# Cutting the last loads of a mean over rows into six runs of columns across two rows, in place of seven within them

## The chip, the cores and the metric

The kernel runs on one core of a Trainium2 chip. The metric is the device time of one execution in microseconds (us). Times below are medians of several executions with their lowest and highest; "span" is the stretch from the first to the last instruction of a profiled execution, some 1.3 us shorter than the time of the same execution.

In the lines of profiles DVE is VectorE, ACT is ScalarE and SPq is the queue of SyncE, which issues the loads; L93 is line 93 of the kernel. A line of a timeline has the start and the length in us, the instruction, and in brackets how long its engine had been idle and what ended that. A **landing** is the moment at which the last semaphore update of a load arrives. Where a landing or a signal is given below to a thousandth, or from "the semaphore updates", it is read from the packed trace (trace.npz): no view prints it.

## The reference

```python
def setup_inputs():
    return {"x": np.random.randn(64, 256, 8192).astype(np.float32)}

def reference(x):
    return np.mean(x, axis=2)
```

These are 16,384 rows of 8192 numbers, 537 MB, read once. The output has 64 KB.

## The kernel before

The rows are taken in 64 blocks. In each, a partition holds two rows next to each other, 16,384 columns or 64 KB, so a block is 8 MB. Three slots in SBUF, the memory on the core, take turns. VectorE sums each block with one instruction. From block 62 on ScalarE helps: it sums the second row of block 62 with an ACTIVATE, its instruction for work element by element, whose accumulator gathers the sum.

Block 63, the last, is loaded in pieces, so that little is left to do when the last bytes come. The first row is one load, the second is cut into six:

```python
LAST_CHUNKS = (4096, 2048, 1024, 512, 256, 256)
ACT_FROM = 512
...
ld = load(xl[:, 0, :], x_l[:, 0, :], tail_sem[0])
dve_sum(head[:, 0:1], xl[:, 0, 0:half])._wait_ge(tail_sem[0], 16)
act_sum(head[:, 1:2], xl[:, 0, half:S])._wait_ge(tail_sem[0], 16)

pos, k = 0, 0
for c, w in enumerate(LAST_CHUNKS):
    last = c == len(LAST_CHUNKS) - 1
    dst = fin_in[:, 0:w] if last else xl[:, 1, pos : pos + w]
    sem = tail_sem[c + 1]
    with tc.issue_after(ld.ins):
        ld = load(dst, x_l[:, 1, pos : pos + w], sem)
    if not last:
        wv = w // 2 if w >= ACT_FROM else w
        # VectorE sums the first wv columns, ScalarE the others, each into
        # a column of fin_in of its own
        ...
```

The last piece goes to `fin_in`, where the partial sums of the second row stand behind it. One **closing sum** over both gives that row's mean. It waits for ScalarE's signal (a drain that raises a semaphore) and for the last landing:

```python
with tc.issue_after(by_act.ins):
    nc.scalar.drain().then_inc(act_sem, 1)
...
scaled_sum(tail_out[:, RUN - R : RUN - 1], head[:])   # the head's scaled sum
...
by_dve = nc.vector.wait_ge(act_sem, 1)
...                                                   # and wait_ge(sem, 16), the last landing
scaled_sum(tail_out[:, RUN - 1 : RUN], fin_in[:, 0 : lastw + k])   # the closing sum
...
last_store = nc.sync.dma_start(out=out_tail, in_=tail_out[:])
```

## Time and profile before

| what | before | from |
|---|---|---|
| time | 1245.04 us (1244.99 to 1245.32, 3 runs) | the runs |
| span | 1244.0 us | page |
| input stream | 536.87 MB at 432 GB/s over the span | page |
| VectorE busy | 1087.1 us, 87% | page |
| start of block 62's sums | 1222.07 us | timeline |
| start of the closing sum | 1241.97 us | timeline |

A trace's absolute times carry all that happened in the 1220 us before. So I measure the end of the kernel as **distances from the start of block 62's sums**, which follow that block's landing by 0.02 us: 1241.97 - 1222.07 = 19.90 us to the closing sum. The last stretch of the chain of waits, whose columns are start, length and what ran:

```profile
1201.94 38.51 DMA xt<-in_x_dram
...
1240.48 1.47 DVE fin_in L93 x3
...
1241.97 0.12 DVE fin_in L99
```

The chain runs over the fourth of the last loads to VectorE's three last short sums and to the closing sum (L99). A chain merges instructions that follow each other closely.

### The profile page before, as it was taken

To read this page: it belongs to the slowest core of one execution; us is meant where nothing else is said; L and a number is where in the kernel's file an instruction comes from. 1 tells how busy PE (TensorE), PEld (TensorE's weight loads), DVE (VectorE), ACT (ScalarE), POOL (GpSimd) and SP (SyncE) were. 2 spreads that over 40 slices of the span, in tenths; PEclk is the share of its full clock that TensorE was granted. 3 is DMA by queue.
4 is the path that set the end of the run, shared out by engine and by line. 5 is a ranking of instruction groups with operands and counts; after the bars stand their busy time and mean duration, and the time that the engine had idled before them with its cause. 6 is when DMAs were issued, how large, how long until landed. Compare 5 with 4: busy or idle time off the path is not lost.

```text
span 1244.0 us, 207 instructions
## 1 busy us (share of the span) xinstructions
PE 0.6 (0%) x2; PEld 0.2 (0%) x2; DVE 1087.1 (87%) x76; ACT 16.4 (1%) x13; POOL 0.7 (0%) x6
## 2 busy tenths in 40 slices
PE   0000000000000000000000000000000000000000
PEld 0000000000000000000000000000000000000000
DVE  2898988989889889898898988989889898898988
ACT  0000000000000000000000000000000000000004
POOL 0000000000000000000000000000000000000000
DMA  9999999999999999999999999999999999999998
GB/s 436 407 438 438 438 438 436 407 438 438 438 438 438 436 407 438 438 438 438 438 436 407 438 438 438 438 438 436 407 438 438 438 438 438 434 411 436 438 438 373
DMA packets 10295, 536.95 MB, mean 432 GB/s; under 512 B 1278, under 2 KB 1590, under 8 KB 1846
## 3 DMA queue, kind: packets, MB, share of 16 engines
q1 hardware_dynamic: 10294, 536.94, 99.9%
q14 instruction: 1, 0.01, 0.0%
HBM read 536.87 MB, written 0.07 MB: 432 GB/s over the span
## 4 chain that ended last, share of the span: by engine, by line
DMA 70%; DVE 29%; SPq 0%; issue 0%; DVEq 0%
DMA xt<-in_x_dram 70%; DVE res L93 26%; DVE tail L93 3%; DVE fin_in L93 0%; SPq L83 0%; DVEq L188 0%; DVE fin_in L99 0%
## 5 line engine op out<-in xcount | busy, mean ns | idle before, releaser
L93 DVE TENSOR_REDUCE res<-xt 128x2 f32<-128x16384 f32 x56 | 964.4, 17221 | 139.4 <-DMA xt<-in_x_dram 139.4
L93 DVE TENSOR_REDUCE tail<-xt 128x2 f32<-128x16384 f32 (+1 forms) x7 | 112.0, 16001 | 13.8 <-DMA xt<-in_x_dram 13.8
L96 ACT ACT_TABLE_LOAD x1 | 1.3, 1283 | 1181.3 <-DVE tail L93 1181.3
L96 ACT ACTIVATE xt<-xt 128x8192 f32<-128x8192 f32 (+5 forms) x6 | 14.7, 2443 | 43.9 <-DMA xt<-in_x_dram 43.7
L93 DVE TENSOR_REDUCE fin_in<-xt 128x1 f32<-128x256 f32 (+3 forms) x5 | 5.0, 1006 | 0.5 <-DMA xt<-in_x_dram 0.4
L93 DVE TENSOR_REDUCE head<-xt 128x1 f32<-128x4096 f32 x1 | 4.4, 4420 | 0.7 <-DMA xt<-in_x_dram 0.7
L160 PE MATMUL ps<-ident,res 128*56 128x128 f32 x2 | 0.6, 404 | 1104.0 <-DVE res L93 1104.0
L96 ACT ACTIVATION_READ_ACCUMULATOR xt<-xt 128x1 f32 x6 | 1.1, 186 | 0.0
L161 DVE TENSOR_SCALAR bulk<-ps 56x128 f32<-56x128 f32 x2 | 0.5, 284 | 0.6 <-PE ps L160 0.6
L99 DVE TENSOR_SCALAR_CACHE_REDUCE fin_in<-fin_in 128x265 f32<-128x265 f32 x1 | 0.4, 431 | 0.0
L160 PEld LDWEIGHTS ps<-ident,res 128*56 128x56 f32 x2 | 0.2, 129 | 1104.0 <-issue 1104.0
L65 POOL TENSOR_SCALAR_AFFINE_SELECT ident<-ident 128x128 f32<-128x128 f32 x1 | 0.3, 292 | 0.1
L99 DVE TENSOR_SCALAR_CACHE_REDUCE head<-head 128x2 f32<-128x2 f32 x1 | 0.2, 155 | 0.1
L164 DVE TENSOR_SCALAR tail_out<-tail 128x14 f32<-128x14 f32 x1 | 0.2, 175 | 0.1
L64 POOL MEMSET ident<- 128x128 f32 x1 | 0.2, 204 | 0.3 <-POOLq L283 0.3
L283 POOL MEMSET const-bfloat16-1.0<- 128x1 bf16 x1 | 0.1, 101 | 0.0
L283 POOL MEMSET const-uint8-127<- 128x1 uint8 x1 | 0.1, 101 | 0.0
L283 POOL MEMSET const-float32-0.0<- 128x1 f32 x1 | 0.1, 98 | 0.2 <-issue 0.2
L283 POOL MEMSET const-float32-1.0<- 128x1 f32 x1 | 0.1, 98 | 0.0
L99 DVE DVE_READ_ACCUMULATOR head<-head 128x1 f32 x1 | 0.1, 84 | 0.0
L99 DVE DVE_READ_ACCUMULATOR fin_in<-fin_in 128x1 f32 x1 | 0.1, 83 | 0.0
## 6 DMA issues: line engine op xcount, KB each, us to landing
xt<-in_x_dram SPq DMA_DIRECT2D x1, 4096.0 KB, 31.1
xt<-in_x_dram SPq DMA_DIRECT2D x1, 2048.0 KB, 35.7
xt<-in_x_dram SPq DMA_DIRECT2D x1, 1024.0 KB, 37.7
xt<-in_x_dram SPq DMA_DIRECT2D x63, 40.8
xt<-in_x_dram SPq DMA_DIRECT2D x1, 512.0 KB, 38.5
xt<-in_x_dram SPq DMA_DIRECT2D x1, 256.0 KB, 38.7
xt<-in_x_dram SPq DMA_DIRECT2D x1, 128.0 KB, 38.6
fin_in<-in_x_dram SPq DMA_DIRECT2D x1, 128.0 KB, 38.5
```

Of the source, the lines that this page charges most:

```text
L64: nc.gpsimd.memset(ident[:], 0.0)
L65: nc.gpsimd.affine_select(out=ident[:], in_=ident[:], compare_op=mybir.AluOpType.not_equal, fill=1.0, base=0, pattern=[[-1, P]], channel_m ...
L93: return untracked(nc.vector.tensor_reduce(out=dst, in_=src, axis=X, op=ADD))
L96: return untracked(nc.scalar.activation(out=src, in_=src, func=COPY, accum_out=dst))
L99: return nc.vector.tensor_scalar(out=src, in0=src, scalar1=inv, scalar2=None, op0=mybir.AluOpType.mult, op1=ADD, accum_out=dst,)
L160: nc.tensor.transpose(out=ps[:TB, :], in_=res[:, r, :], identity=ident[:])
L161: nc.vector.tensor_scalar_mul(out=bulk[:TB, :, r], in0=ps[:TB, :], scalar1=inv)
L164: nc.vector.tensor_scalar_mul(out=tail_out[:, 0 : RUN - R], in0=tail[:], scalar1=inv)
L283: nc = _bacc.Bacc("TRN2", target_bir_lowering=False, num_devices=1)
```

## The change

The last block is cut as one run of 16,384 columns over both rows. The first of six pieces takes the first row whole and 960 columns of the second. A second number for each piece now says how many columns are VectorE's, and VectorE's share is smaller than before. The intent is one load less and less for VectorE to do at the end.

```diff
-LAST_CHUNKS = (4096, 2048, 1024, 512, 256, 256)
-
-ACT_FROM = 512
+LAST_CHUNKS = ((9152, 960), (3968, 1984), (1792, 896), (896, 256), (320, 320), (256, 256))
+HEAD = 3072
 ...
-    x_l = x_t[LB - TB]
-    ld = load(xl[:, 0, :], x_l[:, 0, :], tail_sem[0])
-    dve_sum(head[:, 0:1], xl[:, 0, 0:half])._wait_ge(tail_sem[0], 16)
-    act_sum(head[:, 1:2], xl[:, 0, half:S])._wait_ge(tail_sem[0], 16)
 ...
+        if c == 0:
+            dve_sum(head[:, 0:1], xl[:, 0:HEAD])._wait_ge(sem, 16)
+            act_sum(head[:, 1:2], xl[:, HEAD:S])._wait_ge(sem, 16)
+            assert wv == w - S
+        part = fin_in[:, lastw + k : lastw + k + 2]
+        mid = pos - w + (S if c == 0 else 0) + wv
+        dve_sum(part[:, 0:1], xl[:, mid - wv : mid])._wait_ge(sem, 16)
+        k += 1
+        if mid < pos:
+            by_act = act_sum(part[:, 1:2], xl[:, mid:pos])
 ...
```

More of the change, by code (lines that the diff above doesn't have):

```diff
@@ L39 @@
     TB = NB - RUN // R
-    assert SLOTS <= TB <= P and sum(LAST_CHUNKS) == S
+    assert SLOTS <= TB <= P and sum(w for w, _ in LAST_CHUNKS) == R * S
     inv = 1.0 / float(S)
-    half = S // 2
     x_f = x.rearrange("b c s -> (b c) s")
@@ L57 @@
     act_sem = tc.alloc_semaphore("act")
-    tail_sem = [tc.alloc_semaphore(f"tail{i}") for i in range(len(LAST_CHUNKS) + 1)]
+    tail_sem = [tc.alloc_semaphore(f"tail{i}") for i in range(len(LAST_CHUNKS))]
     res = pool.tile([P, R, TB], F32)
@@ L124 @@
     nparts = 2 * len(LAST_CHUNKS)
-    lastw = LAST_CHUNKS[-1]
-    xl = slots[LB % SLOTS]
+    lastw = LAST_CHUNKS[-1][0]
+    xl = slots[LB % SLOTS][:].rearrange("p r s -> p (r s)")
+    x_l = x_t[LB - TB].rearrange("p r s -> p (r s)")
     fin_in = nc.alloc_sbuf_tensor("fin_in", [P, lastw + nparts], F32)
     head = pool.tile([P, 2], F32)
-    x_l = x_t[LB - TB]
-    ld = load(xl[:, 0, :], x_l[:, 0, :], tail_sem[0])
-    dve_sum(head[:, 0:1], xl[:, 0, 0:half])._wait_ge(tail_sem[0], 16)
-    act_sum(head[:, 1:2], xl[:, 0, half:S])._wait_ge(tail_sem[0], 16)
     pos, k = 0, 0
-    for c, w in enumerate(LAST_CHUNKS):
+    for c, (w, wv) in enumerate(LAST_CHUNKS):
+        sem = tail_sem[c]
         last = c == len(LAST_CHUNKS) - 1
-        dst = fin_in[:, 0:w] if last else xl[:, 1, pos : pos + w]
-        sem = tail_sem[c + 1]
+        dst = fin_in[:, 0:w] if last else xl[:, pos : pos + w]
         with tc.issue_after(ld.ins):
-            ld = load(dst, x_l[:, 1, pos : pos + w], sem)
-        if not last:
-            wv = w // 2 if w >= ACT_FROM else w
-            part = fin_in[:, lastw + k : lastw + k + 2]
-            dve_sum(part[:, 0:1], xl[:, 1, pos : pos + wv])._wait_ge(sem, 16)
-            k += 1
-            if wv < w:
-                by_act = act_sum(part[:, 1:2], xl[:, 1, pos + wv : pos + w])
-                by_act._wait_ge(sem, 16)
-                tc.add_to_no_dep_group("act", by_act.ins)
-                k += 1
-        pos += w
+            ld = load(dst, x_l[:, pos : pos + w], sem)
+        pos += w
+        if last:
+            break
+        if c == 0:
[8 more added lines that the diff above has]
+            by_act = act_sum(part[:, 1:2], xl[:, mid:pos])
+            by_act._wait_ge(sem, 16)
+            tc.add_to_no_dep_group("act", by_act.ins)
+            k += 1
     with tc.issue_after(by_act.ins):
```

## The prediction

> **What bounds the kernel now.** I read the page first (busy shares, the 40 slices, the issues with their landing times), then the chain of waits for the last 60 us, then the timeline of the last 22 us. On the page these lines matter:
>
> ```profile
> DVE  2898988989889889898898988989889898898988
> ...
> GB/s 436 407 438 438 438 438 436 407 438 438 438 438 438 436 407 438 438 438 438 438 436 407 438 438 438 438 438 436 407 438 438 438 438 438 434 411 436 438 438 373
> ...
> HBM read 536.87 MB, written 0.07 MB: 432 GB/s over the span
> ...
> L93 DVE TENSOR_REDUCE res<-xt 128x2 f32<-128x16384 f32 x56 | 964.4, 17221 | 139.4 <-DMA xt<-in_x_dram 139.4
> ```
>
> The input stream runs at 436 to 438 GB/s in nearly every slice and never rests, while VectorE waits before each of its 56 large sums: 139.4 us of idle, all put down to the load (the first 21.8 us of it is the start). The load stream bounds the kernel. The change touches only the last block of 16,384 columns, which is 1/64 of it. Everything up to the landing of the block before it is built as now; the first of the last loads is issued when a slot is freed at 1200.62 us, far ahead of its turn. So the question is only the distance from the landing of the last whole block to the last store.
>
> ```profile
> xt<-in_x_dram SPq DMA_DIRECT2D x1, 4096.0 KB, 31.1
> xt<-in_x_dram SPq DMA_DIRECT2D x1, 2048.0 KB, 35.7
> xt<-in_x_dram SPq DMA_DIRECT2D x1, 1024.0 KB, 37.7
> ...
> xt<-in_x_dram SPq DMA_DIRECT2D x1, 512.0 KB, 38.5
> xt<-in_x_dram SPq DMA_DIRECT2D x1, 256.0 KB, 38.7
> xt<-in_x_dram SPq DMA_DIRECT2D x1, 128.0 KB, 38.6
> fin_in<-in_x_dram SPq DMA_DIRECT2D x1, 128.0 KB, 38.5
> ```
>
> These seven are issued within 3 us and then wait 31 to 39 us for their turn: issue time is hidden altogether. In the timeline:
>
> ```profile
> 1222.07 7.03 ACT L96 ACTIVATE xt<-xt 128x8192 f32<-128x8192 f32 x1 [39.46 <-DMA xt<-in_x_dram]
> ...
> 1231.79 3.62 ACT L96 ACTIVATE xt<-xt 128x4096 f32<-128x4096 f32 x1 [2.60 <-DMA xt<-in_x_dram]
> 1231.79 4.42 DVE L93 TENSOR_REDUCE head<-xt 128x1 f32<-128x4096 f32 x1 [0.75 <-DMA xt<-in_x_dram]
> ...
> 1236.35 0.15 DVE L99 TENSOR_SCALAR_CACHE_REDUCE head<-head 128x2 f32<-128x2 f32 x1
> ...
> 1236.69 2.29 DVE L93 TENSOR_REDUCE fin_in<-xt 128x1 f32<-128x2048 f32 x1 [0.18 <-DMA xt<-in_x_dram]
> ...
> 1241.52 0.42 DVE L93 TENSOR_REDUCE fin_in<-xt 128x1 f32<-128x256 f32 x1
> 1241.97 0.43 DVE L99 TENSOR_SCALAR_CACHE_REDUCE fin_in<-fin_in 128x265 f32<-128x265 f32 x1
> 1242.33 0.08 DVE L99 DVE_READ_ACCUMULATOR fin_in<-fin_in 128x1 f32 x1
> 1242.44 0.36 SPq L182 DMA_DIRECT2D out_dram<-tail_out  x1
> ```
>
> Each number at the left is a start in us. An engine starts some 0.02 us after the landing that it waits for, so landings can be read off: block 62 at 1222.05, the row at 1231.77, then 1236.67, 1239.17 and 1240.45 (the starts at 1236.69, 1239.19 and 1240.48). The last three, issued at about 1202.4, 1202.9 and 1203.36, land by the page at 1241.1, 1241.5 and 1241.86. The closing sum starts at 1241.97: after the last landing at 1241.86, and after VectorE's last short sum ends at 1241.94. **So the stream and VectorE are tied at the end to within 0.1 us.** From that start to the end of the span are 2.03 us (1244.0 - 1241.97): the sum, the store and its landing. The change doesn't touch those.
>
> **What the Trainium skill says.** "DMA: Bandwidth & Descriptors", section Specifications, gives a fabric ceiling of 435 GB/s for the 16 engines. The trace agrees: 438 GB/s in an undisturbed slice, and 8.389 MB in 19.36 us (433 GB/s) between two block landings. The same page, section "Anatomy of one DMA", splits a transfer into a fixed part of about 2 us, mostly the receipt of the last write, and bytes over 436 GB/s. The trace shows that fixed part hidden where loads stand behind each other: 7 loads took 1241.86 - 1222.05 = 19.81 us, and 16,384 columns at the block rate (below) are 19.28, so each load adds 0.076 us. "VectorE: DVE Perf Modes", the section on the TRN2 errata, says that an operation on SBUF pays a fixed latency for every instruction, measured there as about 150 cycles, and the section on perf-mode tiers gives tensor_reduce no fast mode. The trace agrees: 8192, 4096, 2048, 1024, 512 and 256 columns took 8686, 4420, 2286, 1220, 686 and 420 ns, which is 153 + 1.0417 per column. For ScalarE (7030, 3616, 1910, 1057, 629, 416 ns) I fit 203 + 0.8333 per column, and its accumulator read ends some 0.09 us after the ACTIVATE.
>
> **The change part by part.**
>
> *The stream.* It takes away one load and moves no byte less. With a fixed 0.076 us per load, a block of one load in 19.36 us gives (19.36 - 0.08)/16,384 = 1.177 ns per column. Starting from 1222.05, the new landings are: 9152 columns 10.77 + 0.08, at 1232.89; 3968 columns 4.67 + 0.08, at 1237.64; 1792 at 1239.82; 896 at 1240.95; 320 at 1241.41; 256 at 1241.79. Only the last one can set the end, and it comes 0.07 us earlier than now. That is all that the stream gives.
>
> *VectorE.* The first piece now lands 1.12 us later than the row did, so both engines begin later. In exchange VectorE gets 3072 + 960 + 1984 + 896 + 256 + 320 = 7488 columns in six sums in place of 8192 in six: 704 columns less, 0.73 us less. Step by step: 3072 columns take 3.35 us, 1232.91 to 1236.26; 960 take 1.15, to 1237.4; the scaled sum of the two head parts waits for ScalarE (below), some 0.2 us, to about 1237.75; 1984 columns take 2.22, to 1239.97; 896 take 1.09, to 1241.05; 256 take 0.42, to 1241.45; 320 (landed 1241.41) take 0.49, to 1241.91. The closing sum has 264 columns in place of 265 (8 parts, not 9): no change. Now VectorE is done at 1241.94; afterwards at about 1241.91.
>
> *ScalarE.* It has 5120 + 1984 + 896 + 640 = 8640 columns in four instructions in place of 7936 in five. 5120 take 4.47 us from 1232.91, and with the read are done at 1237.47; 1984 from 1237.66 are done at 1239.6; 896 from 1239.84 at 1240.9; 640 from 1240.97 take 0.74 and are done at 1241.80. Now it is done at 1241.66. The signal to VectorE follows through a drain whose length no view here shows; at 0.1 us (my assumption) it is there by 1241.9.
>
> *The sum.* The last landing moves from 1241.86 to 1241.79, VectorE from 1241.94 to 1241.91, ScalarE's signal from about 1241.76 to 1241.90. The closing sum starts after the last of them, at about 1241.94 in place of 1241.97. The gain is 0.03 us, less than the 0.33 us between the three runs of before (1244.99 to 1245.32). I predict **1245.0 us**, against 1245.04.
>
> **The rivals.**
>
> 1. *The head's scaled sum stands ahead of the 960-column sum on VectorE.* The order of instructions on an engine isn't simply the program's: in the trace the head's scaled sum, written after the loop, stands directly behind the head sum. Now that costs nothing, because ScalarE's half ends (1235.5) before VectorE's (1236.21). After the change ScalarE's part ends at 1237.47, 1.2 us after VectorE's 3072 columns. Were the order kept, VectorE would idle there to 1237.55, and all that follows would run late: 1.15 + 2.22 + 1.09 + 0.42 + 0.49 from about 1237.75 ends near 1243.05, so the kernel takes 1.1 us longer, some 1246.1. Against it: the 960-column sum has its data with the head's, comes earlier in the program, and ready work ought to be placed ahead of work that still waits. I give it about one in seven.
>
> 2. *ScalarE becomes the bound.* Its last part has grown from 256 to 640 columns. If its drain takes 0.3 us in place of 0.1, the closing sum starts at 1242.1 to 1242.2: the time is 1245.2. For it: its slack is the smallest of the three. It can't be large, as now the signal is there no later than 0.31 us after the read (1241.66 to 1241.97).
>
> 3. *The pieces flow at another rate.* The new pieces begin at odd offsets (column 9152 is byte 36,608 of a row pair) and all but the last are of other lengths than before; should the stream lose 5% from the second piece on (7232 columns, 8.5 us), it costs 0.4 us, some 1245.4. Against it: in the old pieces, from 128 KB to 4 MB, the rate was the same to within what 0.076 us per load explains. The opposite, that each load saved is worth more than 0.076 us (a full completion wait), is refuted by the landings just read.
>
> No route leads to 2% (25 us): the whole stretch from the last whole block's landing to the end is 1244.0 - 1222.05 = 22 us, 19.3 of which are bytes that must come anyway.
>
> **Range and chances.** The small terms (stream, engines, drain) make 1244.9 to 1245.3, the scatter of runs adds some 0.2 to 0.4 either way, and rival 1 alone lies outside. So 1244.5 to 1245.8 should hold it 8 times in 10. Faster by over 2%: 0.003; slower by over 2%: 0.007, for something not thought of; within 2%: 0.99.
>
> **What would show it right or wrong.** The 4 steps show as follows. The landing of the first piece: a start of VectorE and ScalarE at about 1232.9 us, 10.85 after block 62's; the last load lands 19.74 us after block 62, not 19.81. The durations: 3353, 1153, 2220, 1086, 420 and 486 ns on VectorE and 4470, 1856, 950 and 736 on ScalarE. The order: the 960-column sum directly behind the 3072-column one, and the head's scaled sum after it with less than 0.3 us of idle. The tie: the closing sum within 0.15 us of 19.9 us after block 62's landing. An idle gap of over 1 us on VectorE between its first and second sum of the block, a stretch between two landings over 3% longer than its columns times 1.177 ns plus 0.076 us, or a closing sum held over 0.2 us behind both VectorE's last sum and the last landing would prove the corresponding step wrong.

## The result and the profile after

| | before | after |
|---|---|---|
| time, same rounds | 1245.03 us (1244.93 to 1245.32, 6 runs) | 1245.10 us (1244.84 to 1245.65, 6 runs) |
| span | 1244.0 | 1243.5 |
| start of block 62's sums | 1222.07 | 1221.66 |
| first landing's sums after that | 9.72 | 10.85 |
| closing sum after that | 19.90 | 19.89 |
| store issued after that | 20.37 | 20.36 |

The ratio is 1.0001, with a 95% interval of 0.9988 to 1.0013. A ratio here is the mean time of one kernel's runs over that of the other's in the same rounds, so not quite the ratio of the medians.

The span fell by 0.5 us, but 0.41 of it lies before block 62's sums, where both kernels execute the same instructions. It is scatter of the stream. The rest lies in the last store, which took 1.5 us to land in this trace of before, and 1.4 after and in the repeat of before. In the 13 traces the start of block 62's sums lies anywhere from 1221.60 to 1222.30 us. The distance from there to the closing sum repeats to 0.01 us in both kernels (below), so that is the measure for all that follows.

The issues on the changed kernel's page (size, then us from issue to landing):

```profile
xt<-in_x_dram SPq DMA_DIRECT2D x1, 4576.0 KB, 32.3
xt<-in_x_dram SPq DMA_DIRECT2D x1, 1984.0 KB, 36.7
...
xt<-in_x_dram SPq DMA_DIRECT2D x1, 896.0 KB, 38.4
xt<-in_x_dram SPq DMA_DIRECT2D x1, 448.0 KB, 39.0
xt<-in_x_dram SPq DMA_DIRECT2D x1, 160.0 KB, 39.0
fin_in<-in_x_dram SPq DMA_DIRECT2D x1, 128.0 KB, 38.8
```

There are six loads, issued as early as the seven were, so issue time is hidden as before. Its timeline:

```profile
1232.51 4.47 ACT L96 ACTIVATE xt<-xt 128x5120 f32<-128x5120 f32 x1 [3.73 <-DMA xt<-in_x_dram]
1232.51 3.35 DVE L93 TENSOR_REDUCE head<-xt 128x1 f32<-128x3072 f32 x1 [1.88 <-DMA xt<-in_x_dram]
1235.78 1.14 DVE L93 TENSOR_REDUCE fin_in<-xt 128x1 f32<-128x960 f32 x1
...
1237.11 0.15 DVE L99 TENSOR_SCALAR_CACHE_REDUCE head<-head 128x2 f32<-128x2 f32 x1 [0.18 <-ACT xt L96]
...
1240.58 0.74 ACT L96 ACTIVATE xt<-xt 128x640 f32<-128x640 f32 x1
...
1241.03 0.49 DVE L93 TENSOR_REDUCE fin_in<-xt 128x1 f32<-128x320 f32 x1
...
1241.55 0.43 DVE L99 TENSOR_SCALAR_CACHE_REDUCE fin_in<-fin_in 128x264 f32<-128x264 f32 x1
```

Both engines wait longer for the first piece: 1.88 us on VectorE in place of 0.75. The 960-column sum stands directly behind the head's, and the head's scaled sum comes after it with 0.18 us of idle. Two lines decide the end. The 320-column sum starts at 1241.03: the sum ahead of it started at 1240.58, took 0.42 and ended at 1241.00, and the 320 columns, issued at 1202.00, landed at about 1241.0 (39.0 us on the page; 1241.002 by the semaphore updates). As a sum whose data are there starts before the one ahead has ended (shown below), it is the landing that set this start. ScalarE's 640 columns end at 1240.58 + 0.74 = 1241.32.

Where did the stream's gain go? The first 16,128 columns of the block are there in both kernels when VectorE's last short sum starts. In before, with six loads, that sum starts 1241.52 - 1222.07 = 19.45 us after block 62's; after, with five loads, 1241.03 - 1221.66 = 19.37. So the stream is **0.08 us** ahead. But that sum has 320 columns in place of 256 and takes 0.486 us in place of 0.420, which is **0.07 us** more. It leaves 0.01. What held the end wasn't the last landing: by the semaphore updates it comes at 1241.815 in before (19.75) and at 1241.315 after (19.66), 0.16 and 0.24 us ahead of the closing sum. That isn't all slack, as a wait needs time too: where ScalarE's signal came last (e_four_pieces below), 0.10 us passed from its semaphore update to the closing sum. If a landing needs as long or longer, the last one had at most some 0.06 us to spare in before and 0.14 after (an estimate from these figures).

My theory then: the end is the **landing of the last piece but one and one short sum on VectorE**, with ScalarE's signal close by. The rivals: VectorE's total work sets the end (it has no slack); or the stream's last landing does, and with it the number of loads.

### The profile page after: what moved, and what is told of

Its sections match the earlier page's. It is cut to its first block, busy times and chain, and to the rows that moved or that the text cites. A ratio compares the mean times of both kernels' runs of the same rounds, so it can differ in the third digit from the quotient of the medians.

```text
span 1243.5 us, 204 instructions
## 1 busy us (share of the span) xinstructions
PE 0.6 (0%) x2; PEld 0.2 (0%) x2; DVE 1086.3 (87%) x76; ACT 16.8 (1%) x11; POOL 0.7 (0%) x6
## 4 chain that ended last, share of the span: by engine, by line
DMA 70%; DVE 29%; issue 0%; SPq 0%; DVEq 0%
DMA xt<-in_x_dram 70%; DVE res L93 26%; DVE tail L93 3%; SPq L83 0%; DVE fin_in L93 0%; DVEq L188 0%; DVE fin_in L99 0%
## 5 line engine op out<-in xcount | busy, mean ns | idle before, releaser
L96 ACT ACTIVATE xt<-xt 128x8192 f32<-128x8192 f32 (+4 forms) x5 | 15.0, 3009 | 43.7 <-DMA xt<-in_x_dram 43.6
L93 DVE TENSOR_REDUCE fin_in<-xt 128x1 f32<-128x960 f32 (+4 forms) x5 | 5.3, 1071 | 0.1
L93 DVE TENSOR_REDUCE head<-xt 128x1 f32<-128x3072 f32 x1 | 3.4, 3352 | 1.9 <-DMA xt<-in_x_dram 1.9
```

The lines of the kernel that those rows point to most:

```text
L93: return untracked(nc.vector.tensor_reduce(out=dst, in_=src, axis=X, op=ADD))
L96: return untracked(nc.scalar.activation(out=src, in_=src, func=COPY, accum_out=dst))
```

## The experiments

Eleven kernels ran on the chip, each correct. Here is what they came to; "distance" is from the start of block 62's sums to that of the closing sum.

| kernel | distance | time, us | before in the same rounds |
|---|---|---|---|
| before_again | 19.90 | 1245.04 (1 run) | 1245.24 |
| after_again | 19.89 | 1245.24 | 1245.24 |
| e_head_first | 20.54 | 1245.70 | 1245.24 |
| e_even_split | 20.46 | 1245.86 | 1245.23 |
| e_eight_cuts | 20.77 | 1245.92 | 1245.24 |
| e_four_cuts | 20.03 | 1245.16 (1 run) | 1245.06 |
| e_two_cuts | 19.90 | 1245.00 | 1245.06 |
| e_act_late | 20.04 | 1245.63 (1 run) | 1245.23 |
| e_aligned | 19.97 | 1245.20 | 1245.23 |
| e_four_pieces | 21.13 | 1246.33 | 1245.23 |
| e_retuned | 19.83 | 1245.08 | 1245.06 |

### Both kernels again

No edit. Expected of the kernel before:

> The kernel before, once more, for the scatter of the measure used below: the distance from the start of block 62's sums to the start of the closing sum on VectorE, 19.90 us in its first trace (1241.97 - 1222.07). Theory (the end of the kernel is fixed by the last block alone, and the absolute times differ by the stream before it): again 19.87 to 19.93, while the start of block 62's sums itself may move by some tenths. Rival (the tail itself scatters by tenths): outside of that, and then no difference of 0.01 us between the two kernels means anything.

Expected of the changed one:

> The changed kernel once more, timed in five rounds. Theory: the distance from block 62's sums to the closing sum is 19.89 again (19.86 to 19.92), the last load lands 19.6 to 19.75 after them, and the time is within 0.3 us of before. Rival (the last landing's move shows in the time): faster by 0.1 us or more, in all rounds.

The distances came out as 1241.75 - 1221.85 = 19.90 and 1241.97 - 1222.08 = 19.89, the very values of the first traces, though the starts of block 62's sums had moved by -0.22 and +0.42 us. VectorE's last short sum started at 19.44 and 19.35, so the 0.08 or 0.09 of the stream repeats too. The changed kernel took 1245.24 us (1244.74 to 1245.39, 5 runs) beside 1245.24 (1244.86 to 1245.42, 9 runs), ratio 1.0 (0.9986 to 1.0013). The difference of 0.01 us in the tail is steady in the traces, and no count of rounds here would find it in the time.

### Has VectorE slack? The head's scaled sum ahead of the 960-column sum

```diff
+        if c == 0:
+            head_sum = scaled_sum(tail_out[:, RUN - R : RUN - 1], head[:])
         part = fin_in[:, lastw + k : lastw + k + 2]
 ...
-        dve_sum(part[:, 0:1], xl[:, mid - wv : mid])._wait_ge(sem, 16)
+        with tc.issue_after(head_sum.ins):
+            dve_sum(part[:, 0:1], xl[:, mid - wv : mid])._wait_ge(sem, 16)
 ...      # and the head's scaled sum behind the loop is gone
```

> The changed kernel with the head's scaled sum forced ahead of the 960-column sum on VectorE. Theory (VectorE has next to no slack between the first piece and the end): it idles until ScalarE's 5120 columns are done, some 15.45 us after block 62's sums, and then 1.14 + 2.22 + 1.09 + 0.42 + 0.49 us follow without a gap, so the closing sum starts 20.96 us after block 62's sums, 1.07 later than in the changed kernel; the time rises by about 1.1 us (0.7 to 1.4). Rival (the stream sets the end and VectorE has slack): less than 0.3 us.

Its timeline:

```profile
1237.11 0.15 DVE L99 TENSOR_SCALAR_CACHE_REDUCE head<-head 128x2 f32<-128x2 f32 x1 [1.24 <-ACT xt L96]
...
1237.19 4.99 DVE L93 TENSOR_REDUCE fin_in<-xt 128x1 f32<-128x960 f32 x5
...
1242.21 0.43 DVE L99 TENSOR_SCALAR_CACHE_REDUCE fin_in<-fin_in 128x264 f32<-128x264 f32 x1
```

VectorE idles 1.24 us for ScalarE, as expected, and the 960-column sum starts 15.52 us after block 62's in place of 14.12: 1.40 late. But the closing sum is only 0.65 late (1242.21 - 1221.67 = 20.54), where I had expected 1.07. Both theories missed: VectorE has slack of about three quarters of a us between the first piece and the end.

The lines show where. Five sums fill 4.99 us, while their durations add to 1148 + 2207 + 1075 + 408 + 475 ns = 5.31. Looked at singly, the 1984-column sum starts 0.08 us before the 960-column one ends, and the 896-column one 0.09 before that one ends. A sum whose data are already there starts **0.08 to 0.09 us before the one ahead ends**. The Trainium skill explains such an overlap: its page "Perfetto Trace Analysis", section "Per-instruction lifecycle", says that the reported end of a VectorE instruction includes the acknowledgement of its writes, while the next may begin to fetch when the one ahead has finished executing. The trace agrees with the overlap; that the acknowledgement is its cause isn't shown here. A second part of the room is the head's scaled sum itself: in the changed kernel 1.48 us lie between the starts of the 960-column and the 1984-column sum, here 1.07 (1237.19 to 1238.26), which accounts for 0.41 of the 0.75; the rest is in the sums behind. In the changed kernel four sums from 1237.26 on fill 4.25 us, for durations of 4.21. There each of the four starts 0.02 us after its own landing (1237.234, 1239.424, 1240.559 and 1241.002 by the semaphore updates): its last sums aren't a chain of work but a row of waits, though the chain of waits merges them.

### What the columns moved to ScalarE are worth: VectorE keeps half

```diff
-HEAD = 3072
+HEAD = 4096
-... (896, 256), ...
+... (896, 448), ...
```

> The six new loads with VectorE keeping half of each piece where it had half before: head 4096 and 4096, the 896-column piece 448 and 448 (1216 columns go back from ScalarE to VectorE). Theory (the longer first piece is only free because columns went to ScalarE): VectorE has no gap from the first landing on, 4.42 + 1.14 + 0.2 + 2.22 + 1.09 + 0.62 + 0.49 us, so the closing sum starts 21.07 us after block 62's sums, 1.2 later than in the changed kernel, and the time rises by about 1.2 us. Rival (the stream alone sets the end): under 0.3 us.

1216 columns more on VectorE are 1.27 us at 1.0417 ns each. The closing sum came 0.57 later (1242.37 - 1221.91 = 20.46), half of what I expected, and the time was 1245.86 us beside 1245.23, ratio 1.0005 (0.9988 to 1.0022). It is the same miss: I had put sums end to end and let the head's scaled sum cost 0.2 us. It cost 0.07 here (start of it at 1238.14, of the next sum at 1238.21), and the four sums behind it filled 4.12 us for durations of 4.37 (2215 + 1076 + 608 + 474 ns). The direction holds: the later first landing is free only since columns went to ScalarE.

### What a load costs: the first piece as eight, four and two loads

The engines' instructions stay as they are; only the loads of the first piece are cut, on one semaphore, which both engines await in full.

```diff
 ...
+        for i in range(CUTS if c == 0 else 0):
+            a, b = i * w // CUTS, (i + 1) * w // CUTS
+            with tc.issue_after(ld.ins):
+                ld = load(xl[:, a:b], x_l[:, a:b], sem)
 ...      # and the waits of the first piece are for 16 * CUTS
+CUTS = 8        # then 4, then 2
```

> The changed kernel with its first piece loaded as eight loads of 1144 columns on one semaphore, with the engines' work as it was: seven loads more. Theory (each load adds 0.076 us to the stream): the first piece lands 0.53 us later, 11.38 us after block 62 in place of 10.85, and everything behind it, the closing sum included, comes 0.53 later (20.4). Rival 1 (loads behind each other cost nothing): no move, 19.9. Rival 2 (each load pays a full completion of over 1 us): 7 us or more.

```profile
1233.52 3.35 DVE L94 TENSOR_REDUCE head<-xt 128x1 f32<-128x3072 f32 x1 [2.76 <-DMA xt<-in_x_dram]
```

The first landing came 0.89 us late, not 0.53, and all behind it too (distance 20.77). The time was 1245.92 us (1245.67 to 1246.05), all four runs above all nine of before (1244.86 to 1245.42), though the ratio's interval holds 1 (1.0006, 0.9991 to 1.0021). That is 0.89 / 7 = 0.127 us for each load in the mean. It is neither 0.076 nor nothing nor a whole us, so I ran two more kernels.

The mean hides an event, though. By the semaphore updates the eight loads landed 1.43, 1.43, 1.43, 1.36, 1.37, 1.52, 1.77 and 1.44 us after each other, the first counted from block 62's landing. Each load makes 16 updates, and over the sixth and the seventh the last of the 16 fell back from 0.3 to 0.7 us behind the first. The first one was only 0.48 us late at the end of the piece, 0.07 us for each added load; the other 0.40 us of the 0.89 are that falling back. What caused it isn't known, and one trace doesn't tell whether it belongs to the eight cuts.

> The changed kernel with its first piece as two loads of 4576 columns: one load more, as many as the kernel before has. The eight cuts cost 0.127 us for each added load (0.89 for 7) where 0.076 was expected. Theory 1 (0.076 per load holds for one load, and the eight cuts cost more for their small pieces or their full queue): the first piece lands 10.92 to 10.93 us after block 62's sums, the closing sum starts at 19.96 to 19.97. Theory 2 (a load costs 0.127 us in general): 10.97 to 10.98, and 20.01 to 20.02. The rest moves with the first landing.

> The same with four loads of 2288 columns, three loads more. Theory 1 as above: first landing at 11.07 to 11.08, closing sum at 20.12; theory 2: 11.23 and 20.27. A value between speaks for a cost that grows as the pieces get smaller or as the queue fills.

The first lines of block 63 on VectorE, and the closing sum, with two cuts:

```profile
1232.69 3.35 DVE L94 TENSOR_REDUCE head<-xt 128x1 f32<-128x3072 f32 x1 [1.87 <-DMA xt<-in_x_dram]
...
1241.75 0.43 DVE L100 TENSOR_SCALAR_CACHE_REDUCE fin_in<-fin_in 128x264 f32<-128x264 f32 x1
```

| first piece as | KB each | first landing's sums | per added load | closing sum |
|---|---|---|---|---|
| 1 load (after) | 4576 | 10.85 | | 19.89 |
| 2 loads | 2288 | 10.84 | 0.00 | 19.90 |
| 4 loads | 1144 | 11.00 | 0.05 | 20.03 |
| 8 loads | 572 | 11.74 | 0.127 | 20.77 |

With two loads the kernel has as many as before, and the end moved by 0.01 us. **Both theories fell**: a load doesn't have a fixed cost of 0.076 us. A load more at this size costs nothing that the trace shows; in smaller pieces the mean cost of each is higher. Whether the small size is the cause stays open: with four and eight cuts the issuing queue also stalled (one issue stood for 14.69 us in both), and with eight nearly half of the cost is the event above. The stalled issue with four cuts:

```profile
1204.05 14.69 SPq L84 DMA_DIRECT2D fin_in<-in_x_dram  x1
```

For the change it follows that "one load less" isn't by itself the gain: two cuts have one load more and keep the 19.37 us of the changed kernel for the last short sum's start (1241.22 - 1221.85). The 0.08 us must come from how the rest is cut (before has six pieces of 4096 columns and less, after five). Which of them was not settled; the run with four pieces below puts a small load at 0.065 us, which fits.

### ScalarE's signal: a later end on ScalarE

```diff
-... (896, 256), ...
+... (896, 64), ...
```

> The changed kernel with the 896-column piece split 64 to VectorE and 832 to ScalarE (256 and 640 before). ScalarE is then done about 19.91 us after block 62's sums (19.74 in the changed kernel), VectorE no later than before. Theory (the closing sum waits for ScalarE's drain and signal, some 0.1 us): it starts at 20.0 to 20.1, and the difference to ScalarE's end is the length of drain and signal, which no view showed. Rival 1 (the drain is long, 0.3 us): 20.2 or more. Rival 2 (ScalarE's signal has ample time, only VectorE and the stream count): 19.85 to 19.9.

```profile
1241.21 0.90 ACT L96 ACTIVATE xt<-xt 128x832 f32<-128x832 f32 x1
...
1242.34 0.43 DVE L99 TENSOR_SCALAR_CACHE_REDUCE fin_in<-fin_in 128x264 f32<-128x264 f32 x1 [0.20 <-ACTq L155]
```

The closing sum now waits for ScalarE's queue, and starts at 1242.34 - 1222.30 = 20.04, as the theory expected. ScalarE's ACTIVATE ends at 1241.21 + 0.90 = 1242.11; accumulator read, drain, signal and the wait on VectorE take **0.23 us** from there. Now put this into the changed kernel: 1241.32 + 0.23 = 1241.55, exactly the start of its closing sum. After the change ScalarE's signal and VectorE arrive together. The semaphore updates tell them apart: from the update by ScalarE's signal to the closing sum lie 0.10 us here, in the next two runs, and in the changed kernel too (1241.454 to 1241.553). From the update by VectorE's last sum to the closing sum lie 0.02 us where only VectorE was late (1241.948 to 1241.972 in before), and 0.03 in the changed kernel (1241.523 to 1241.553). So there ScalarE's signal comes last, by some 0.01 us. In before, ScalarE's last ACTIVATE of 256 columns ran from 1241.15 to 1241.57, and its signal was there at about 1241.80, 0.17 us early:

```profile
1241.15 0.42 ACT L96 ACTIVATE xt<-xt 128x256 f32<-128x256 f32 x1
```

### Do odd lengths slow the stream? Pieces in multiples of 128 columns

```diff
-((9152, 960), (3968, 1984), (1792, 896), (896, 256), (320, 320), (256, 256))
+((9216, 1024), (3968, 1984), (1792, 896), (896, 256), (256, 256), (256, 256))
```

> The changed kernel with pieces whose lengths are all multiples of 128 columns: 9216, 3968, 1792, 896, 256, 256, with 1024 columns for VectorE after the head. Theory (offset and length don't change the rate): landings follow 1.177 ns per column and 0.076 us per load, the first at 10.92 us after block 62; the last VectorE sum is 256 and not 320 columns long, so the closing sum starts about 19.83 us after block 62's sums, 0.06 earlier. Rival (the odd offsets slow the stream): the stretches between landings get shorter than that, by 0.2 us or more in all.

The landings fell where expected: the first piece's sums at 10.92 or 10.93 us. So the odd offsets cost nothing that shows. But the closing sum came later, not earlier:

```profile
1240.85 0.74 ACT L96 ACTIVATE xt<-xt 128x640 f32<-128x640 f32 x1
...
1241.83 0.43 DVE L99 TENSOR_SCALAR_CACHE_REDUCE fin_in<-fin_in 128x264 f32<-128x264 f32 x1 [0.18 <-ACTq L155]
```

VectorE was ready at 1241.65, at 19.79, as hoped. Then it waited 0.18 us for ScalarE, whose 640 columns had landed 0.07 us later than in the changed kernel: 1240.85 + 0.74 + 0.24 = 1241.83. The distance is 19.97, and the time 1245.20 us beside 1245.23. I had left ScalarE out of the expectation; the run shows that it binds as soon as VectorE doesn't.

### Fewer loads still: four pieces

```diff
-((9152, 960), (3968, 1984), (1792, 896), (896, 256), (320, 320), (256, 256))
+((9152, 960), (3968, 1984), (3008, 1248), (256, 256))
```

> The changed kernel with four pieces: 9152, 3968, 3008 (1248 on VectorE, 1760 on ScalarE) and 256. Two loads less still. Theory (a load is worth 0.076 us of stream, and what counts is what the engines have left to do after the last large piece): the stream ends 0.15 us earlier, but the 3008 columns land 19.2 us after block 62 and take 1.45 us on VectorE and 1.76 on ScalarE, so the closing sum starts at about 21.1, 1.2 us later than in the changed kernel, and the time rises by about 1.2 us. Rival (fewer loads shorten the end): a start before 19.9 and a faster kernel.

```profile
1237.19 1.86 ACT L96 ACTIVATE xt<-xt 128x1984 f32<-128x1984 f32 x1 [0.18 <-DMA xt<-in_x_dram]
...
1240.83 1.67 ACT L96 ACTIVATE xt<-xt 128x1760 f32<-128x1760 f32 x1 [1.69 <-DMA xt<-in_x_dram]
...
1242.73 0.43 DVE L99 TENSOR_SCALAR_CACHE_REDUCE fin_in<-fin_in 128x261 f32<-128x261 f32 x1 [0.45 <-ACTq L155]
```

The closing sum started at 1242.73 - 1221.60 = 21.13, as expected, and waited 0.45 us for ScalarE, whose 1760 columns ended at 1240.83 + 1.67 = 1242.50, again 0.23 before it. The time was 1246.33 us beside 1245.23. What counts is what the engines have left to do behind the last large piece.

The run also prices a small load. The 3008 columns in one load landed 1240.83 - 1237.19 = 3.64 us after the piece ahead, by the sums that start on the landings; in the changed kernel the same columns in three loads took 1241.03 - 1237.26 = 3.77. Two loads less are 0.13 us, so 0.065 for each.

### The refined theory at work: another cut of the last pieces

```diff
-... (896, 256), (320, 320), (256, 256))
+... (896, 352), (256, 256), (320, 320))
```

> The changed kernel with its last pieces cut otherwise: 896 columns split 352 to VectorE and 544 to ScalarE, then 256 and 320 in place of 320 and 256. The refined theory (the closing sum starts after the later of two: the last but one landing or the sum before it, whichever frees VectorE last, plus one short sum and 0.03 us; and the end of ScalarE's last ACTIVATE plus 0.23 us; a sum whose data are there starts 0.09 us before the one ahead of it ends): the closing sum starts 19.81 us after block 62's sums in place of 19.89, since VectorE is ready at 19.80 and ScalarE's signal at 19.81; but it has 328 columns in place of 264 and takes about 0.495 us in place of 0.428, so its end comes only 0.01 us earlier and the time stays within 0.3 us of before. Rival 1 (something else holds the closing sum): it starts at 19.87 or later. Rival 2 (the gain comes through): faster by 0.1 us in all rounds.

```profile
1240.84 0.66 ACT L96 ACTIVATE xt<-xt 128x544 f32<-128x544 f32 x1
...
1241.74 0.49 DVE L99 TENSOR_SCALAR_CACHE_REDUCE fin_in<-fin_in 128x328 f32<-128x328 f32 x1
...
1242.27 0.36 SPq L182 DMA_DIRECT2D out_dram<-tail_out  x1
```

The closing sum started at 1241.74 - 1221.91 = 19.83, where 19.81 was expected and 19.87 or more would have spoken against. It took 0.494 us for its 328 columns in place of 0.428 for 264. The store was issued at 1242.27 - 1221.91 = 20.36, the same as in the changed kernel (20.36) and 0.01 before the kernel before (20.37). The time was 1245.08 us beside 1245.06, ratio 1.0001 (0.9987 to 1.0015). The 0.06 us gained at the start of the closing sum are paid back within it. No version here beats both kernels.

## Why the prediction was right

The time, 1245.10 us beside 1245.0 predicted, and the verdict were right, and so was the main reason: the stream bounds the kernel, and the change can only move the end of it by hundredths of a us. By its own steps:

- **The stream.** The first landing was predicted 10.85 us after block 62's and came so (10.85 and 10.84). The sums that follow landings directly started within 0.03 us of plan: ScalarE's 1984, 896 and 640 columns at 1237.26, 1239.45 and 1240.58. The last landing, predicted at 19.74 after block 62's, came at 19.68 and 19.67; it set nothing. Of the old one the prediction had 1241.86 from the page, which rounds; the semaphore updates have 1241.815, so its mean for each load should have been 0.070 us and not 0.076. The step behind the gain, "so each load adds 0.076 us", took that mean over seven loads of mixed sizes for a constant. It is not one: 0.00 for a second load of 2288 KB, 0.065 for each of two small ones saved. It predicted the right move of the landings here (0.07 us; the last short sum shows 0.08) with a reason that holds for small loads at most. And that "the trace agrees" with the ceiling of 435 GB/s is so to 1%: the undisturbed slices show 438 (439 after), which is above it.
- **The durations** were right to 0.001 us for all sums but the 960-column one (1.142 us in place of 1.153), and so were those of ScalarE.
- **VectorE.** It was predicted to end at 1241.91 with block 62's sums at 1222.07, so at 19.84; it ended at 1241.51 - 1221.66 = 19.85. That is luck in part: the sum put the work end to end and so found no room, while in truth each short sum waited for its landing, and about 0.75 us of room lay between. The head's scaled sum, put down at 0.2 us of delay, cost none, as the 1984 columns landed just then.
- **The tie.** "The stream and VectorE are tied at the end to within 0.1 us" held in before, where the last landing had at most some 0.06 us to spare. But the landing that counts is the one before it, plus one short sum on VectorE. That is where the gain went: 0.08 us from the stream against 0.07 for 64 more columns in that sum.
- **ScalarE.** Done at 1241.80 in the prediction, or 19.73; measured 1241.22 + 0.18 - 1221.66 = 19.74. The drain assumed at 0.1 us is about 0.15 from the end of the accumulator read (1241.40 to 1241.55). The remark that its slack is the smallest was right: it went from 0.17 us to none.
- **The rivals.** The first did not happen, and forced by hand it cost 0.65 us and not 1.1: the mechanism was right, the term for the sums behind it was too long by 0.08 to 0.09 for each hand-over. The second happened in the small: ScalarE's signal is the last to come, by some 0.01 us, and in the run with aligned pieces it cost 0.18 us. The third is refuted by those pieces, which landed no sooner than their columns say.

## What to carry to other kernels

Where a stream bounds a kernel, as here, cutting the last loads otherwise touches little more than what remains behind the last large landing; for one piece fewer, ask which landing the last instruction truly waits for, and add the work that hangs on that one. Moving columns between engines moves the bound to the other engine's signal, so work out all arrivals (last landing, the one before it with its sum, the other engine's end with its signal) each time. For effects below the scatter of runs, take a distance inside the trace from a point that both kernels share, and don't take a merged chain of instructions for a chain of work.

## What the Trainium skill lacked or had wrong

- "DMA: Bandwidth & Descriptors" gives a fixed part of about 2 us for one transfer issued by GpSimd, and no figure for loads that stand behind each other in one queue, as SyncE issued them here. Its rule of 1 MiB or more per DMA, in the section "Rules for kernel authors", fits what was seen: the added time was 0.00 us for one more load at 2288 KB each, 0.05 for each added at 1144 KB, and 0.127 in the mean at 572 KB, nearly half of it one event.
- No page read says how many loads a queue takes before an issue stalls. With the first piece in four loads the issue of the ninth of the block's loads stood for 14.69 us (from 1204.05), with eight loads that of the ninth too (from 1204.02), and with seven loads in all, as in before, none did. With four, that load still landed 37.5 us after its issue began, behind all others.
- "Perfetto Trace Analysis", section "Per-instruction lifecycle", tells that a reported duration includes the acknowledgement of the writes, but gives no length there. A rough one stands in another section of the page, "Optimizing Scalar/DVE Operations": about 60 ns of overhead for VectorE on SBUF, reported as about twice that because the half for the acknowledgement overlaps with the next instruction. Here a VectorE sum with its data at hand started 0.08 to 0.09 us before the reported end of the one ahead, so durations must not be added up.
- No page read here gives the way from a ScalarE ACTIVATE with an accumulator, over a drain, to a waiting VectorE instruction. It took 0.23 us from the end of the ACTIVATE in the runs where VectorE waited for it (20.04 and 21.13 us), and 0.24 in the third.
